# Attention scores of a hybrid diffusion backbone: 289 contraction rows per key tile packed as 128 + 128 + 33, the 33 in half of the array's rows

## The chip, the cores and the metric

The program runs on one core of one Trainium2 chip. The metric is the device time of one execution in microseconds (us). Five things work side by side on the core, each through its own queue of instructions in a fixed order: TensorE (PE in the profile; its loading of stationary weights is listed apart as PEld), VectorE (DVE), ScalarE (ACT), GpSimd (POOL), and SyncE (SP), which here only issues DMA transfers. Semaphores order them.

## The reference

Two layers (DEPTH 2) of a mixer over 2048 latent and 256 context tokens, width 1024. What matters here is the attention of each layer, 8 heads wide:

```python
q = rms_norm((rms_norm(cq, q_norm_w) @ w_uq).reshape(B, T, 8, 96), q_head_norm_w)      # 64 plain + 32 rotary
k = rms_norm(concat([k_nope, k_rope]), k_head_norm_w)                                   # 64 plain + 32 rotary
s = einsum('bqhd,bkhd->bhqk', q, k) * 96 ** -0.5      # latent queries see 2304 keys, context queries 256
p = softmax(s, axis=-1)
o = einsum('bhqk,bkhd->bqhd', p, v)
```

Before it come the projections of tokens to q, k and v and two gated convolutions; after it the output projection and the residual. In the last layer the context queries are left out.

## The kernel before

The products of this kernel take operands of type fp32r, and an fp32 value is carried as two such parts, hi and lo, so that `a*b` is summed as `hi*hi + hi*lo + lo*hi`. The work of a layer is four functions called one after the other: `tokens` (q, k, v, written to DRAM as `q_d`, `kn_d`, `kr_d`, `v_d`), `features` (the convolutions), `attention`, `project`.

`attention` walks over jobs: head by head, four blocks of 512 latent queries, and in layer 0 one more block of 256 context queries per head. A job walks over pairs of key tiles (a tile is 128 keys): 18 tiles in 9 pairs for a block of latent queries, one pair for a block of context queries. In all there are 584 pairs, 8 x 37 in layer 0 and 8 x 36 in layer 1. One pair does this:

- **scores**, L1073 to L1075: for each of the two key tiles three products into one PSUM bank `sc` (tag "a", three banks): K hi by Q hi over 97 rows (96 dimensions and a row that subtracts the query's maximum), K hi by Q lo over 96 rows, K lo by Q hi over 96 rows. 97 + 96 + 96 = 289 rows of contraction in three products, each 512 columns long (256 for context queries);
- **exponentials**, L1076 and L1077 on ScalarE: `p` in fp32 and `ph` in fp32r; L1078 on GpSimd forms `pl = p - ph`; L1085 on VectorE adds up `p`;
- **products with V**, L1100 and L1101: four per pair, issued one pair later.

Between the pairs stand the products L985 (`pmax`) that find the maxima of the queries of a later job, reduced by VectorE (L986), and, in layer 0, the modulation products of later use: L216 (`pm`), and a transpose of a row of four partitions, L220 (`pt`).

`load(h)` fetches a head: K and Q lie as tiles `[97, 18, 2, 128]` with the hi and the lo part side by side, so that one transfer of long rows on GpSimd's queue serves each of the `kn_d`, `kr_d` and `q_d` pieces. Two buffers alternate between heads; a head's transfers are called two jobs ahead.

The code names operations in a natural order, and a scheduler with a timeline model of its own then sets the order of each engine's queue, within the priorities that the code gives. TensorE runs its products in that order. In the built program each product also carries the part of the 128 x 128 array that it occupies (rows x columns): the whole array for all large products, 128 x 32 for L216 (four output columns) and 32 x 128 for L220 (four rows of contraction).

Of the kernel before, what the change touches and what calls it, by code (L numbers as in the profile page):

```python
# [9 lines left out]
F32 = mybir.dt.float32  # L10
F32R = mybir.dt.float32r
# [7 lines left out]
P = 128  # L19
# [4 lines left out]
NT = SEQ + CTX  # L24
NTT = NT // P
DEPTH = 2
H = 8
NOPE, ROPE, DV, QK = 64, 32, 64, 96
# [56 lines left out]
def trunk(ctx: ExitStack, tc: tile.TileContext, ins, out):  # L85
    nc = tc.nc
    V, S, G, PE = nc.vector, nc.scalar, nc.gpsimd, nc.tensor

    def pool(stack, name, **kw):
        return stack.enter_context(tc.tile_pool(name=name, bufs=kw.pop("bufs", 1), **kw))  # L90
# [5 lines left out]
    def psum(tag, name):  # L96
        return ps.tile([P, 512], F32, tag=tag, name=name, bufs={"a": 3, "b": 2}.get(tag, 1))
# [137 lines left out]
    def tokens(l, start):  # L235
# [353 lines left out]
        for t in range(NTT + 2):  # L589
# [8 lines left out]
            for step in (STEPS, STEPS1)[l]:  # L598
# [340 lines left out]
    def attention(l, start):  # L939
        es = ExitStack()  # L940
        tp = pool(es, f"A{l}", reuse_waits="tile")
        vp = pool(es, f"Av{l}", reuse_waits="tile")
        op = pool(es, f"Ao{l}", reuse_waits="tile", side="right")
        hp = [pool(es, f"Aa{l}", reuse_waits="tile", side="right"), pool(es, f"Ab{l}", reuse_waits="tile")]
# [3 lines left out]
        jobs = []  # L948
# [7 lines left out]
        kv = {}  # L956
        count = [0]

        def load(h):
            K = hp[h % 2].tile([97, NTT, 2, P], F32R, tag="K", name="K")  # L960
            G.dma_start(K[0:NOPE], kn_d[l][h])
            G.dma_start(K[NOPE:97], kr_d[l][h])
            Q = hp[h % 2].tile([97, NTT, 2, P], F32R, tag="Q", name="Q")
            nq_ = (SEQ if last else NT) // P
            G.dma_start(Q[0:QK, :nq_], q_d[l][h, :, :nq_])
            Vt = vp.tile([P, NTT, P], F32R, tag=f"V{h % 2}", name="Vt")
            G.dma_start(Vt, v_d[l][h])
            kv[h] = (K, Vt, Q)

        def prepare(h, s, n, k0):  # L970

            K, Vt, Q = kv[h]
            keys = [(a, min(512, NT - a)) for a in range(k0 * P, NT, 512)]
            m = mx[count[0] % 2]

            early = count[0] < NE
            count[0] += 1

            part = m
            nq = n // P  # L980
            steps = []

            def chunk(t, c, a, w):
                pm = psum("b", "pmax")
                PE.matmul(pm[:, :w], lhsT=Q[0:QK, s // P + t, 0], rhs=K[0:QK, a // P : (a + w) // P, 0], start=True, stop=True)  # L985
                V.tensor_reduce(part[:, t, c : c + 1], pm[:, :w], axis=AX.X, op=ALU.max)  # L986

            def finish():
                V.tensor_reduce(m[:, 0:nq, 96:97], part[:, 0:nq, 0 : len(keys)], axis=AX.X, op=ALU.max, negate=True)

            def turn():
                px = psum("b" if early else "e", "pmt")
                for t in range(nq):
                    PE.matmul(px[0:97, t * P : (t + 1) * P], lhsT=m[:, t, :], rhs=idr, start=True, stop=True)
                S.copy(Q[96:97, s // P : (s + n) // P, 0], px[96:97, :n].rearrange("p (a t) -> p a t", t=P))

# [11 lines left out]
        def ahead(idx, share):  # L1008

            while len(sums) <= idx + 1 and len(sums) <= len(jobs):  # L1010
                steps, ends = [], []
                for j in jobs[len(sums) - 1]:
                    a, finish, turn = prepare(*j)
                    steps += [[st] for st in a]
                    steps[-1].append(finish)
                    ends.append(turn)
                steps[-1] += ends
                queue.extend(steps)
                sums.append(sums[-1] + len(steps))
            if idx < len(jobs):  # L1020
                goal = sums[idx] + round(share * (sums[idx + 1] - sums[idx]))
                while sums[-1] - len(queue) < goal:
                    with tc.high_priority(offset=PO):
                        for st in queue.pop(0):
                            st()

        with start():
            load(0)
            ahead(0, 1)

        ready = []
# [21 lines left out]
        for idx, job in enumerate(jobs):  # L1053
            h = job[0][0]
            if job[0][1] == (1024 if h else 512) and h + 1 < H:
                load(h + 1)
            pairs = [(j, it) for j in job for it in range(j[3], NTT, 2)]
            for pi, ((h, s, n, k0), kt0) in enumerate(pairs):
                if idx == len(jobs) - 1 and pi == len(pairs) - AE:
                    mark = tc.cur_priority  # L1060
                K, Vt, Q = kv[h]
# [7 lines left out]
                scs = []  # L1069
# [240 lines left out]
```

## Time and profile before

| | |
|---|---|
| median of 3 runs | 3695.93 us (3688.89 to 3696.3) |
| the profiled execution's own time | 3695.0 us |
| its span, first to last instruction | 3693.2 us |
| PE busy | 3529.8 us (96%) |
| DVE busy | 2888.8 us (78%) |
| POOL busy | 2341.6 us (63%) |
| ACT busy | 2166.7 us (59%) |
| mean granted clock of TensorE | 0.978 |
| attention, layer 0 | about 812 to 1737 us |
| attention, layer 1 | about 2599 to 3500 us |

Busy time is the union of an engine's instruction spans. Matmuls are pipelined and their ends are modelled, so a span of 0.40 us of a product with 512 columns overlaps the next one: what a product costs in a full queue is the distance from its start to the next start. The start of a row PEld is the moment at which the weights of that product begin to be loaded.

### The profile page before, as it was taken

To read this page: it belongs to the slowest core of one execution; us is meant where nothing else is said; L and a number is where in the kernel's file an instruction comes from. 1 tells how busy PE (TensorE), PEld (TensorE's weight loads), DVE (VectorE), ACT (ScalarE), POOL (GpSimd) and SP (SyncE) were. 2 spreads that over 40 slices of the span, in tenths; PEclk is the share of its full clock that TensorE was granted. 3 is DMA by queue.
4 is the path that set the end of the run, shared out by engine and by line. 5 is a ranking of instruction groups with operands and counts; after the bars stand their busy time and mean duration, and the time that the engine had idled before them with its cause. 6 is when DMAs were issued, how large, how long until landed. Compare 5 with 4: busy or idle time off the path is not lost. (4 is left out here: it accounts for less than half of the span.)

```text
span 3693.2 us, 52810 instructions
## 1 busy us (share of the span) xinstructions
PE 3529.8 (96%) x17532; PEld 2916.9 (79%) x17532; DVE 2888.8 (78%) x5472; ACT 2166.7 (59%) x4328; POOL 2341.6 (63%) x1497
## 2 busy tenths in 40 slices
PE   7899999999999999999999989999999999998999
PEld 5787888887888787877788878887777777776777
DVE  5986977877888888888437878769988888888832
ACT  4665343247778777877445663433677777776720
POOL 4664344348888888877435654444687887877721
PEclk8999999999999999999999999999999999999999
DMA  7567333433333213312776773435232202222163
GB/s 219 171 186 205 82 107 110 113 112 78 79 79 88 61 45 82 85 58 64 232 231 207 215 213 100 114 99 125 80 76 61 41 27 61 59 61 75 43 197 114
DMA packets 394386, 411.47 MB, mean 111 GB/s; under 512 B 19168, under 2 KB 332128, under 8 KB 388960
## 3 DMA queue, kind: packets, MB, share of 16 engines
q1 hardware_dynamic: 387712, 333.87, 31.2%
q0 software_dynamic: 6400, 74.22, 8.9%
q8 instruction: 138, 2.26, 0.3%
q14 instruction: 136, 1.11, 0.1%
HBM read 266.72 MB, written 141.59 MB: 111 GB/s over the span
## 5 line engine op out<-in xcount | busy, mean ns | idle before, releaser
L1078 POOL TENSOR_TENSOR pl<-p,ph 128x1024 fp32r<-128x1024 f32 (+1 forms) x584 | 1387.2, 2397 | 276.2 <-ACT ph L1077 110.4
L986 DVE TENSOR_REDUCE mx<-pmax 128x1 fp32r<-128x512 f32 (+1 forms) x1296 | 795.1, 628 | 122.0 <-PE pmax L985 113.6
L1076 ACT ACTIVATE p<-sc 128x512 f32<-128x512 f32 x1168 | 713.4, 612 | 240.5 <-PE sc L1075 232.7
L1085 DVE TENSOR_TENSOR acc<-acc,p 128x512 f32<-128x512 f32 x1096 | 756.7, 690 | 55.9 <-ACT p L1076 29.5
L1077 ACT ACTIVATE ph<-sc 128x512 fp32r<-128x512 f32 x1168 | 703.8, 612 | 20.1 <-PE po L1100 16.2
L194 PE MATMUL pf<-hhf,wh 128*128 128x256 f32 (+1 forms) x1584 | 549.3, 348 | 18.2 <-ACT tg L867 8.4
L196 PE MATMUL pf<-hhf,wl 128*128 128x512 f32 (+1 forms) x1584 | 546.4, 347 | 4.5 <-POOL wl L191 3.7
L195 PE MATMUL pf<-hlf,wh 128*128 128x256 f32 (+1 forms) x1584 | 547.2, 346 | 0.0
L985 PE MATMUL pmax<-K,Q 96*128 96x512 f32 (+1 forms) x1296 | 465.0, 386 | 34.8 <-DVE mx L986 26.8
L1073 PE MATMUL sc<-Q,K 97*128 97x512 f32 x1168 | 476.5, 408 | 11.7 <-ACT ph L1077 9.3
L1101 PE MATMUL po<-pl,Vt 128*128 128x512 f32 x1168 | 467.9, 401 | 2.1 <-POOL pl L1078 1.8
L1074 PE MATMUL sc<-Q,K 96*128 96x512 f32 x1168 | 465.2, 398 | 0.0
L1100 PE MATMUL po<-ph,Vt 128*128 128x512 f32 x1168 | 461.9, 396 | 1.1 <-DMA Vt<-v_d 0.8
L1075 PE MATMUL sc<-Q,K 96*128 96x512 f32 x1168 | 462.4, 396 | 0.0
L191 POOL TENSOR_TENSOR wl<-wraw,wh 128x1024 fp32r<-128x1024 f32 x104 | 253.8, 2441 | 292.8 <-ACT wh L190 279.4
L747 DVE SCALAR_TENSOR_TENSOR cacc<-z,hv,cacc 128x384 f32<-128x384 f32 (+5 forms) x780 | 403.0, 561 | 14.3 <-ACT cacc L742 11.2
L194 PEld LDWEIGHTS pf<-hhf,wh 128*128 128x128 f32 x1584 | 303.7, 192 | 57.2 <-ACT wh L190 9.1
L196 PEld LDWEIGHTS pf<-hhf,wl 128*128 128x128 f32 x1584 | 303.0, 192 | 44.3 <-POOL wl L191 7.2
L985 PEld LDWEIGHTS pmax<-K,Q 96*128 96x128 f32 x1296 | 245.3, 190 | 116.9 <-DVE mx L986 58.6
L195 PEld LDWEIGHTS pf<-hlf,wh 128*128 128x128 f32 x1584 | 303.8, 192 | 36.1
L1073 PEld LDWEIGHTS sc<-Q,K 97*128 97x128 f32 x1168 | 222.2, 190 | 71.3 <-ACT ph L1077 20.0
L1075 PEld LDWEIGHTS sc<-Q,K 96*128 96x128 f32 x1168 | 224.5, 192 | 51.5
(257 smaller groups left out, 6189.0 us busy)
## 6 DMA issues: line engine op xcount, KB each, us to landing
wraw<-in_w_in SPq DMA_DIRECT2D x108, 512.0 KB
q_d<-sg SPq DMA_DIRECT2D x68, 384.0 KB
wm<-in_w_mod SPq DMA_DIRECT2D x46, 512.0 KB
v_d<-vs SPq DMA_DIRECT2D x36, 512.0 KB
kn_d<-sg SPq DMA_DIRECT2D x72, 256.0 KB
K<-kn_d POOLq DMA_DIRECT2D x16, 1152.0 KB, 8.5
Vt<-v_d POOLq DMA_DIRECT2D x16, 1152.0 KB, 14.8
o_d<-o SPq DMA_DIRECT2D x64, 256.0 KB
```

Of the source, the lines that this page charges most:

```text
L194: PE.matmul(out_, lhsT=ahi, rhs=bhi, start=first, stop=False)
L195: PE.matmul(out_, lhsT=ahi, rhs=blo, start=False, stop=False)
L196: PE.matmul(out_, lhsT=alo, rhs=bhi, start=False, stop=last)
L985: PE.matmul(pm[:, :w], lhsT=Q[0:QK, s // P + t, 0], rhs=K[0:QK, a // P : (a + w) // P, 0], start=True, stop=True)
L986: V.tensor_reduce(part[:, t, c : c + 1], pm[:, :w], axis=AX.X, op=ALU.max)
L1073: PE.matmul(sc[:, :n], lhsT=K[0:97, kt, 0], rhs=Q[0:97, qt, 0], start=True, stop=False)
L1075: PE.matmul(sc[:, :n], lhsT=K[0:QK, kt, 1], rhs=Q[0:QK, qt, 0], start=False, stop=True)
L1076: S.activation(p[:, z, :n], sc[:, :n], AF.Exp, scale=scale)
L1077: S.activation(ph[:, z, :n], sc[:, :n], AF.Exp, scale=scale)
L1078: G.tensor_tensor(pl[:, :, :n], p[:, :, :n], ph[:, :, :n].bitcast(F32), op=ALU.subtract)
L1085: V.tensor_tensor(acc[:, :n], acc[:, :n], p[:, z, :n], op=ALU.add)
L1101: PE.matmul(po[:, :n], lhsT=Vt[:, kt0 + z, :], rhs=pl[:, z, :n], start=False, stop=final and z == 1)
```

## The change

Per key tile the 289 rows are packed as two products over all 128 rows of the array (L1106) and a rest of 33 or 34 rows. For that the tiles K and Q become `[128, 18, 2, 128]`: their two planes hold two packed sets of rows instead of hi and lo. The rests of the two tiles of a pair lie in a new tile KC, that of the even tile on partitions 0 to 32 and that of the odd tile on partitions 64 to 97; the even one's partner is a new tile `qc` of 33 rows, the odd one's lies in Q. The two rests, L1102 and L1103, are given the two halves of the array's rows (64 x 128 at row 0 and at row 64) and two PSUM banks, and they open the two score sums. There are as many products as before (six per pair).

`load(h)` now copies rows to their places with 20 transfers of 512-byte pieces on SyncE's queue (16 to Q and K, 4 to KC), and a block of queries has two more for `qc`; V stays on GpSimd's queue. The row of ones becomes ones in the hi plane and zeros in the lo plane.

```diff
-            K = hp[h % 2].tile([97, NTT, 2, P], F32R, tag="K", name="K")
-            G.dma_start(K[0:NOPE], kn_d[l][h])
-            G.dma_start(K[NOPE:97], kr_d[l][h])
-            Q = hp[h % 2].tile([97, NTT, 2, P], F32R, tag="Q", name="Q")
+            K = hp[h % 2].tile([P, NTT, 2, P], F32R, tag="K", name="K")
+            KC = vp.tile([98, NTT // 2, P], F32R, tag=f"KC{h % 2}", name="KC")
+            Q = hp[h % 2].tile([P, NTT, 2, P], F32R, tag="Q", name="Q")
...
+            for r0, src, z in ((0, kn[0:63], 0), (64, kr[0:33], 0), (97, kn[63:64], 0), (63, kn[30:31], 0), (98, kn[0:30], 0)):
+                ld(k[r0 : r0 + src.shape[0], :, 0], src[:, :, z])
...
+            for r0, src, z in ((0, kr[0:32], 0), (32, kn[63:64], 0), (64, kr[0:33], 1), (97, kn[63:64], 1)):
+                ld(c[r0 : r0 + src.shape[0]], odd(src[:, :, 1])[:, :, z])
             G.dma_start(Vt, v_d[l][h])
...
+        def load_qc(h, s, n):
+
+            t = tp.tile([33, 4, P], F32R, tag="qc", name="qc", bufs=3)
+            a, e = s // P, (s + n) // P
+            nc.sync.dma_start(t.bitcast(F32)[0:32, : e - a], q_d[l][h, 64:96, a:e, 0])
+            nc.sync.dma_start(t.bitcast(F32)[32:33, : e - a], q_d[l][h, 63:64, a:e, 0])
+            qc[h, s] = t
...
-                PE.matmul(pm[:, :w], lhsT=Q[0:QK, s // P + t, 0], rhs=K[0:QK, a // P : (a + w) // P, 0], start=True, stop=True)
+                PE.matmul(pm[:, :w], lhsT=Q[:, s // P + t, 0], rhs=K[:, a // P : (a + w) // P, 0], start=True, stop=True)
...
-                for z in range(2):
-                    kt, qt = kt0 + z, slice(s // P, (s + n) // P)
-                    sc = psum("a", "sc")
-                    PE.matmul(sc[:, :n], lhsT=K[0:97, kt, 0], rhs=Q[0:97, qt, 0], start=True, stop=False)
-                    PE.matmul(sc[:, :n], lhsT=K[0:QK, kt, 0], rhs=Q[0:QK, qt, 1], start=False, stop=False)
-                    PE.matmul(sc[:, :n], lhsT=K[0:QK, kt, 1], rhs=Q[0:QK, qt, 0], start=False, stop=True)
+                scs = [psum("a", "sc") for _ in range(2)]
+                C = KC[:, kt0 // 2]
+                PE.matmul(scs[0][:, :n], lhsT=C[0:33], rhs=qc[h, s][:, : n // P], start=True, stop=False, tile_position=(0, 0))
+                PE.matmul(scs[1][:, :n], lhsT=C[64:98], rhs=Q[64:98, qt, 0], start=True, stop=False, tile_position=(64, 0))
+                for z, sc in enumerate(scs):
+                    for i in range(2):
+                        PE.matmul(sc[:, :n], lhsT=K[:, kt0 + z, i], rhs=Q[:, qt, i], start=False, stop=i == 1)
```

The scheduler sets the order anew. On TensorE, in the middle of layer 0's attention, this stands before (`sc` scores, `po` products with V, `pmax` maxima of a later job):

```order
L1073 MATMUL sc<-Q,K 128x512
L1074 MATMUL sc<-Q,K 128x512
L1075 MATMUL sc<-Q,K 128x512
L1073 MATMUL sc<-Q,K 128x512
L1074 MATMUL sc<-Q,K 128x512
L1075 MATMUL sc<-Q,K 128x512
L1101 MATMUL po<-pl,Vt 128x512
L1100 MATMUL po<-ph,Vt 128x512
L1101 MATMUL po<-pl,Vt 128x512
L1100 MATMUL po<-ph,Vt 128x512
L985 MATMUL pmax<-K,Q 128x256
```

and this after, in the middle of layer 0's attention too:

```order
L1103 MATMUL sc<-Q,KC 128x512
L1106 MATMUL sc<-Q,K 128x512 x2
L1012 MATMUL pmax<-K,Q 128x512
L1102 MATMUL sc<-qc,KC 128x512
L1106 MATMUL sc<-Q,K 128x512 x2
L1132 MATMUL po<-pl,Vt 128x512
L1131 MATMUL po<-ph,Vt 128x512
L1132 MATMUL po<-pl,Vt 128x512
L1131 MATMUL po<-ph,Vt 128x512
L1103 MATMUL sc<-Q,KC 128x512
L1106 MATMUL sc<-Q,K 128x512 x2
```

Each rest stands in front of the two full products of its own tile. Over the whole queue of TensorE, 29 of the 584 pairs have their two rests next to each other; the other 555 pairs have them apart, with products of the whole array on either side of each.

The second place is the start of attention in layer 1 on TensorE, where the last work of `features` (`pf`, and the layer norm and pointwise products `pmu`, `pva`, `ppw`) is still under way. Before:

```order
L985 MATMUL pmax<-K,Q 128x512
L985 MATMUL pmax<-K,Q 128x256
L1073 MATMUL sc<-Q,K 128x512
L1074 MATMUL sc<-Q,K 128x512
L1075 MATMUL sc<-Q,K 128x512
L196 MATMUL pf<-hhf,wl 128x512
L194 MATMUL pf<-hhf,wh 128x512
L195 MATMUL pf<-hlf,wh 128x512
```

After:

```order
L769 MATMUL pva<-tl,onr 128x264
L769 MATMUL pva<-th,onr 128x264
L769 MATMUL pva<-tl,onr 128x264
L1021 MATMUL pmt<-idr,mx_90 97x128 x4
L1012 MATMUL pmax<-K,Q 128x512 x4
L1102 MATMUL sc<-qc,KC 128x512
L1103 MATMUL sc<-Q,KC 128x512
L1106 MATMUL sc<-Q,K 128x512 x4
```

The first score of the layer moved from ahead of the last `pf` products to behind the last `pva` product.

## Rows read from the trace of the kernel before

**Rows 1.** The page: span and parts 1 (busy us, share, instructions) and 2.

```profile
span 3693.2 us, 52810 instructions
...
PE 3529.8 (96%) x17532; PEld 2916.9 (79%) x17532; DVE 2888.8 (78%) x5472; ACT 2166.7 (59%) x4328; POOL 2341.6 (63%) x1497
...
PEclk8999999999999999999999999999999999999999
```

**Rows 2.** Busy time in two stretches of attention, layer 0 and layer 1.

```profile
core 0: us, PE busy (x) PEld busy (x) DVE busy (x) ACT busy (x) POOL busy (x), PEclk, DMA share, GB/s
820.00:1660.00 840.00, 827.26 (x4063) 663.51 (x4062) 726.03 (x1338) 648.61 (x1220) 723.66 (x331) 0.99 0.30 75
2600.00:3440.00 840.00, 815.78 (x3554) 645.27 (x3553) 736.55 (x1241) 621.68 (x1184) 663.55 (x305) 0.99 0.25 59
```

**Rows 3.** PE's groups in one head of layer 0, 937.85 to 1050.62 us, shapes apart.

```profile
line engine op names shapes xcount | busy us, mean ns | idle before us <-releasers
L1073 PE MATMUL sc<-Q,K 97*128 97x512 f32 x72 | 29.3, 408 | 0.0
...
L985 PE MATMUL pmax<-K,Q 96*128 96x512 f32 x64 | 24.6, 405 | 0.1
```

**Rows 4.** Timeline of PE around a transpose L220 in layer 0's attention.

```profile
start us, us, engine line op out<-in xcount [idle before <-releaser]
1050.14 0.40 PE L985 MATMUL pmax<-K,Q 96*128 96x512 f32 x1
1050.47 0.22 PE L220 MATMUL pt<-idr,mrow 4*128 4x4 f32 x1
1050.62 0.50 PE L1073 MATMUL sc<-Q,K 97*128 97x512 f32 x1
1050.96 0.40 PE L1074 MATMUL sc<-Q,K 96*128 96x512 f32 x1
1051.19 0.40 PE L1075 MATMUL sc<-Q,K 96*128 96x512 f32 x1
1051.42 0.40 PE L1073 MATMUL sc<-Q,K 97*128 97x512 f32 x1
```

**Rows 5.** Timeline of PEld, the weight loads of the same stretch.

```profile
1050.47 0.13 PEld L220 LDWEIGHTS pt<-idr,mrow 4*128 4x128 f32 x1 [0.37 <-issue]
1050.62 0.19 PEld L1073 LDWEIGHTS sc<-Q,K 97*128 97x128 f32 x1
1050.73 0.19 PEld L1074 LDWEIGHTS sc<-Q,K 96*128 96x128 f32 x1
1050.96 0.19 PEld L1075 LDWEIGHTS sc<-Q,K 96*128 96x128 f32 x1
```

**Rows 6.** Timeline of PEld, four loads of L220 behind one another.

```profile
49.72 0.32 PEld L220 LDWEIGHTS pt<-idr,mrow 4*128 4x128 f32 x4
```

**Rows 7.** Timeline of PE, from whole-array products to L216 in fp32r parts.

```profile
1020.51 0.40 PE L1101 MATMUL po<-pl,Vt 128*128 128x512 f32 x1
1020.75 0.22 PE L216 MATMUL pm<-wmh,s 128*4 128x128 f32 x1
```

**Rows 8.** Timeline of PEld, the same stretch and where it ends.

```profile
1020.52 0.08 PEld L216 LDWEIGHTS pm<-wmh,s 128*4 128x4 f32 x1
...
1021.59 0.08 PEld L216 LDWEIGHTS pm<-wml,s 128*4 128x4 f32 x1
1021.65 0.19 PEld L985 LDWEIGHTS pmax<-K,Q 96*128 96x128 f32 x1
```

**Rows 9.** Timeline of PEld at the start, L216 in plain fp32 between `ptok` products.

```profile
45.22 0.19 PEld L195 LDWEIGHTS ptok<-wt_lo,hh 128*128 128x128 f32 x1 [0.22 <-issue]
45.61 0.09 PEld L216 LDWEIGHTS pm<-wm,rinv 128*4 128x4 f32 x2 [0.20 <-issue]
45.92 0.19 PEld L196 LDWEIGHTS ptok<-wt_hi,hl 128*128 128x128 f32 x1 [0.22 <-issue]
```

**Rows 10.** DMA queues: packets, MB, share of 16 engines' span; an issue, us to landing.

```profile
q1 hardware_dynamic: 387712, 333.87, 31.2%
...
Q<-q_d POOLq DMA_DIRECT2D x8, 1728.0 KB, 21.1
```

**Rows 11.** Issue of a transfer of 1024 pieces of 512 bytes on SP, line L203.

```profile
L203 SPq DMA_DIRECT2D wm<-in_w_mod x38: 367/384/1875, 31.6 to 1560.3; - x38
```

**Rows 12.** Timeline of PE at the start of layer 1's attention.

```profile
2598.83 0.40 PE L1073 MATMUL sc<-Q,K 97*128 97x512 f32 x1
```

**Rows 13.** Timeline of DVE there, the first step behind the `pva` products.

```profile
2621.02 0.42 DVE L782 TENSOR_SCALAR cva<-pva 128x264 f32<-128x264 f32 x1
```

More of the change, by code (lines that the diff above doesn't have):

```diff
@@ L959, in load @@
         def load(h):
-            K = hp[h % 2].tile([97, NTT, 2, P], F32R, tag="K", name="K")
-            G.dma_start(K[0:NOPE], kn_d[l][h])
-            G.dma_start(K[NOPE:97], kr_d[l][h])
-            Q = hp[h % 2].tile([97, NTT, 2, P], F32R, tag="Q", name="Q")
+            K = hp[h % 2].tile([P, NTT, 2, P], F32R, tag="K", name="K")
+            KC = vp.tile([98, NTT // 2, P], F32R, tag=f"KC{h % 2}", name="KC")
+            Q = hp[h % 2].tile([P, NTT, 2, P], F32R, tag="Q", name="Q")
+            Vt = vp.tile([P, NTT, P], F32R, tag=f"V{h % 2}", name="Vt")
@@ L964, in load @@
             nq_ = (SEQ if last else NT) // P
-            G.dma_start(Q[0:QK, :nq_], q_d[l][h, :, :nq_])
-            Vt = vp.tile([P, NTT, P], F32R, tag=f"V{h % 2}", name="Vt")
-            G.dma_start(Vt, v_d[l][h])
-            kv[h] = (K, Vt, Q)
+            k, c, q = K.bitcast(F32), KC.bitcast(F32), Q.bitcast(F32)
+            kn, kr, qd = kn_d[l][h], kr_d[l][h], q_d[l][h, :, :nq_]
+            odd = lambda d: d.rearrange("d (n two) t -> d n two t", two=2)
+            ld = nc.sync.dma_start
@@ new lines, in load @@
+            for r0, src, z in ((0, qd[0:63], 0), (64, qd[64:96], 0), (97, qd[63:64], 0), (63, qd[30:31], 1), (98, qd[0:30], 1), (96, kr[ROPE : ROPE + 1, :nq_], 1)):
+                ld(q[r0 : r0 + src.shape[0], :nq_, 0], src[:, :, z])
+            for r0, src, z in ((0, kn[0:63], 0), (64, kr[0:33], 0), (97, kn[63:64], 0), (63, kn[30:31], 0), (98, kn[0:30], 0)):
+                ld(k[r0 : r0 + src.shape[0], :, 0], src[:, :, z])
+            for r0, src, z in ((0, qd[31:96], 1), (65, qd[0:63], 0)):
+                ld(q[r0 : r0 + src.shape[0], :nq_, 1], src[:, :, z])
@@ new lines, in load @@
+            for r0, src, z in ((0, kn[31:64], 0), (33, kr[0:32], 0), (65, kn[0:63], 1)):
+                ld(k[r0 : r0 + src.shape[0], :, 1], src[:, :, z])
+            for r0, src, z in ((0, kr[0:32], 0), (32, kn[63:64], 0), (64, kr[0:33], 1), (97, kn[63:64], 1)):
+                ld(c[r0 : r0 + src.shape[0]], odd(src[:, :, 1])[:, :, z])
+            G.dma_start(Vt, v_d[l][h])
+            kv[h] = (K, Vt, Q, KC)
+        def load_qc(h, s, n):
[4 more added lines that the diff above has]
+            qc[h, s] = t
@@ L970, in prepare @@
+        qc = {}
         def prepare(h, s, n, k0):
-            K, Vt, Q = kv[h]
+            K, Vt, Q, _ = kv[h]
             keys = [(a, min(512, NT - a)) for a in range(k0 * P, NT, 512)]
@@ L1028, in attention @@
             load(0)
+            load_qc(*jobs[0][0][:3])
             ahead(0, 1)
@@ L1056, in attention @@
                 load(h + 1)
+            for j in jobs[idx][1:] + jobs[idx + 1 : idx + 2][0][:1] if idx + 1 < len(jobs) else jobs[idx][1:]:
+                load_qc(*j[:3])
             pairs = [(j, it) for j in job for it in range(j[3], NTT, 2)]
@@ L1060, in attention @@
                     mark = tc.cur_priority
-                K, Vt, Q = kv[h]
+                K, Vt, Q, KC = kv[h]
                 first, final = kt0 == k0, kt0 == NTT - 2
@@ L1068, in attention @@
                 pl = tp.tile([P, 2, 512], F32R, tag="pl", name="pl", bufs=3)
-                scs = []
-                for z in range(2):
-                    kt, qt = kt0 + z, slice(s // P, (s + n) // P)
-                    sc = psum("a", "sc")
-                    PE.matmul(sc[:, :n], lhsT=K[0:97, kt, 0], rhs=Q[0:97, qt, 0], start=True, stop=False)
-                    PE.matmul(sc[:, :n], lhsT=K[0:QK, kt, 0], rhs=Q[0:QK, qt, 1], start=False, stop=False)
-                    PE.matmul(sc[:, :n], lhsT=K[0:QK, kt, 1], rhs=Q[0:QK, qt, 0], start=False, stop=True)
+                qt = slice(s // P, (s + n) // P)
+                scs = [psum("a", "sc") for _ in range(2)]
[5 more added lines that the diff above has]
+                        PE.matmul(sc[:, :n], lhsT=K[:, kt0 + z, i], rhs=Q[:, qt, i], start=False, stop=i == 1)
                     S.activation(p[:, z, :n], sc[:, :n], AF.Exp, scale=scale)
@@ L1298 @@
     arrays["idn"] = np.eye(P, dtype=f)
-    arrays["one"] = np.ones((H, 2 * NT), f)
+    arrays["one"] = np.ascontiguousarray(np.broadcast_to(np.array([1, 0], f)[None, None, :, None], (H, NTT, 2, P)).reshape(H, 2 * NT))
     nc = bacc.Bacc("TRN2", target_bir_lowering=False, num_devices=1)
```

## The prediction

> **What bounds the kernel now.** I read first the page's span and parts 1 and 2 [rows 1]: TensorE is busy 96% of the span at a granted clock near full, the next engine, VectorE, 78%. The change touches attention alone, so the second view is the busy time in a stretch of each layer's attention [rows 2]: PE works 827.3 of 840 us in layer 0 and 815.8 of 840 in layer 1; VectorE 726 and 737, GpSimd 724 and 664, ScalarE less. The third is PE's groups within one head of layer 0 [rows 3]: before 72 score products and 64 maxima products it stood idle 0.0 and 0.1 us. So in attention PE's queue is the path, and it runs dry for 12.7 + 24.2 = 37 us in 1680. Whatever a pair gains or loses on PE is gained or lost in the time. The price of one product is the distance between starts: 1050.96, 1051.19, 1051.42, so 0.23 us for 512 columns [rows 4].
>
> **What the change removes.** Not a product: six per pair before, six after. The gain can only come from the two rests of a pair streaming at the same time, which would turn 6 x 0.23 into 5 x 0.23. For that they must follow each other on PE. In the order above they do in 29 of 584 pairs; in the other 555 a rest stands alone between products of the whole array. So 1110 rests can gain nothing, and what decides is what it costs to go from products of all 128 rows to a product in a 64-row part, and back.
>
> **The price of one visit to a row part.** The kernel before has such visits, though not for this type and size: L220, a transpose in plain fp32 that occupies 32 of the array's rows. Between whole products a load of weights normally starts with the product before it, so it is hidden: L1075's load starts at 1050.96, the start of L1074 [rows 4, 5]. Around L220 this stops. Its load starts at 1050.47, 0.33 after the start of L985 (1050.14), that is 0.10 after that product's 0.23 of streaming are over; L1073's load starts 0.15 after L220's; and L1073's load lies bare, since the next load, which starts when L1073 begins to stream, comes 0.11 later (1050.62 to 1050.73) [rows 4, 5]. From L985 to L1074 it takes 0.82 us, where two whole products take 0.46: the visit costs 0.36 us (0.35 unrounded at the least) with four columns in it. A rest has 512 columns, which add the 0.23 that it also cost before. Thus a lone rest costs 0.36 more than the product that it replaces.
>
> One part of it is open: L220's weights load fast, four of them in 0.32 us with the last one 0.13, so (0.32 - 0.13) / 3 = 0.06 each [rows 6]; the rest's are fp32r over 128 columns like L1073's, whose load took 0.11 [rows 5]. That is up to 0.05 more, so 0.35 to 0.41. I take 0.37, near the low end, because rows 6 are the only loads into a row part.
>
> The Trainium skill, "TensorEngine Tiling (Array Packing)", section "Tiling Modes", says that changing the tiling mode, not just the tile, drains TensorE. It gives no price. Rows 5 agree; rows 8 do not, as the third rival tells. By that sentence the sum is the one below; without it, that of the third rival.
>
> **The sum.**
> - 1110 lone rests x 0.37 = +411 us (0.35: 388; 0.41: 455). PE is the path, so all of it lies on it; VectorE, ScalarE and GpSimd merely get slack.
> - 29 pairs with adjacent rests: one visit, +0.37, and between nothing and 0.23 back if the two stream together; at 0.12 back, 29 x 0.25 = +7 (4 to 12).
> - PE's dry spells, 37 us in 1680 [rows 2], about 40 over both attentions, mostly waits for slower neighbours: with PE slower they shrink. I take -25 (-40 to 0).
> - The start of attention in layer 1: the first score, before at 2598.83 [rows 12], now stands behind the last `pva` product, whose result VectorE takes at 2621.02 [rows 13]. At most 22 us for PE, but `features`' own chain, then free of attention's work on VectorE, ends sooner; I take half, +11. Layer 0's start moves in the same way over less work; I take nothing, and up to another 22 for the range. So +11 (0 to 44).
> - The maxima products take 128 rows instead of 96: as many columns, the same 0.23; 0.
> - The loads. A head is now 256 x 18 pieces each for Q and K, 67 x 9 for KC and 33 x 18 for `qc`, some 10,400 pieces of 512 bytes. At the mean of the hardware queue, 0.312 x 16 x 3693 / 387,712 = 0.048 us of an engine each [rows 10], that is 31 us of all 16 engines per head, where Q alone took 21 to land before. A head lasts 112.8 us (rows 3's stretch) and the DMA engines are at 0.25 to 0.30 of their time [rows 2]. In SP's order the transfers for a head stand where its buffers come free, a whole head before their use. So they are hidden: 0. Without that cover it would be up to 31 us a head. Issuing 20 + 8 transfers at 0.38 [rows 11] takes SP 11 us per head; behind them wait only stores of results, which nobody needs before `project`. GpSimd's queue loses three issues a head, which is no bound.
>
> 411 + 7 - 25 + 11 = +404. On the profiled execution's 3695.0 us (span 3693.2, median of the runs 3695.9, so the same to 0.03%) this gives 4099: **4100 us**, 11% slower. The ends of the terms give 352 to 511, so 4047 to 4206.
>
> **The rivals.**
>
> *Second: the loads lie bare, but nothing waits for the array to run empty.* Then a visit costs the rest's load, 0.06 to 0.11, and L1106's, 0.11 [rows 5, 6]: 0.17 to 0.22 on 1139 visits, 194 to 251, middle 222. 222 - 25 + 11 = +208: 3903 (3850 to 3990). For it: L220 is plain fp32, and the 0.10 behind the stream may belong to that type. Against: loads hidden under streaming is what whole products do, so something holds the load back until the stream has ended, and that something would also hold the 0.10.
>
> *Third, the other side: changing to a row part is free for fp32r.* L216 occupies a 128 x 32 part. With fp32r parts its load starts at 1020.52, a full 0.23 ahead of its product at 1020.75, with the start of L1101 [rows 7, 8], and L985's load follows the last of them by 0.06: no stop in either direction. In plain fp32 the same line L216 does stop: its load comes 0.39 after that of a `ptok` product of 416 columns (45.22 to 45.61), and the load after two of them 0.31 later (45.61 to 45.92), where loads between whole products are never bare [rows 9]. So a stop has been seen for plain fp32 alone, in a column part and in a row part; for fp32r only a column part is on record, and it is free. If the type decides and not the part, a lone rest costs its 0.23 as before: 3695 - 29 x 0.23 + 11 = 3699 (3688 to 3732), not slower where the starts cost under 14 us. Against: a column part leaves all rows of the array in use, so that weights can be loaded as ever; a row part changes what the moving data feed, and L220 is the only row part here.
>
> *Fourth: the change does what it says.* 584 x 0.23 = 134 us less: 3695 - 134 + 11 = 3572. The Trainium skill, "TensorE: Matmul & The Clock Gate", section "Part 3: Packing small matmuls — row/col tiling", measured four row tiles at 3.07 times the speed of one; that is this mechanism. But PE runs products in the order of its queue, and there the partners stand apart.
>
> *Fifth: more than the visits.* If the stops lowered the granted clock of the stages, now 0.99 [rows 2], every product there would be dearer too: over 4200.
>
> **How the numbers follow.** First case 0.56, second 0.15, third 0.22, fourth 0.03, fifth 0.04. The time is that of the first, 4100. Alone it would reach from 4047 to 4206; with 0.44 elsewhere the range must take in the second case and the upper half of the third: 3700 to 4200, which leaves out the fourth, the fifth and half of the third. A measurement of this kernel can tell about 0.2%, or 7 us, from no change. Slower by more: first, second, fifth and half of the third, 0.86. Faster by more: the fourth and a little of the third, 0.06. Within: the remainder of the third, 0.08.
>
> **What would show it.** In the trace after: the loads of L1102 and L1103 some 0.33 us behind the start of the product before them (first case), 0.23 (second) or with it (third); the first L1106's load bare behind the rest; a head of layer 0 lasting 112.8 + 72 x 0.37 = 139 us; VectorE's share of attention falling from 0.87 to about 0.72; PE never waiting for a DMA of K, Q, KC or `qc`. The prediction is wrong if the rests' loads start with the product before them, or if PE waits for loads, which would add to any case.

## The result and the profile after

The changed kernel takes 4126.89 us (median of 4 runs, 4124.92 to 4138.65) against 3695.44 us (4 runs, 3688.89 to 3696.3): a ratio of 1.118, 95% interval 1.116 to 1.120. It is 431 us slower; forecast were 404 and 4100 us, so the sum is 27 us short. The profiled execution of the changed kernel took 4138.65 us, the slowest of its four, so readings of it add up to some 12 us more than the medians differ by.

The page of the changed kernel, span, part 1 and the clock's row of part 2, against [rows 1]:

```profile
span 4136.9 us, 53464 instructions
...
PE 3966.5 (96%) x17532; PEld 2838.2 (69%) x17532; DVE 2910.1 (70%) x5472; ACT 2232.8 (54%) x4328; POOL 2318.6 (56%) x1449
...
PEclk8999999989999999999999999997999999999999
```

As many products as before, PE as full as before, every other engine with nearly the same busy time in a longer span. So PE's queue is still the path and each turn through it lasts longer. Besides the first slice, the clock's row has two that fell below 9, an 8 and a 7; before it had none. They come back below, at the starts of attention.

Two stretches of attention, one in each layer, against [rows 2] (columns: the stretch, its length, busy time and instructions of PE, PEld, DVE, ACT and POOL, granted clock, share of the DMA engines, GB/s):

```profile
900.00:1700.00 800.00, 797.81 (x3232) 491.15 (x3231) 581.87 (x1053) 540.04 (x973) 568.83 (x246) 1.00 0.30 70
2850.00:3700.00 850.00, 844.82 (x2930) 501.79 (x2929) 606.04 (x1017) 540.29 (x978) 542.40 (x233) 0.98 0.26 60
```

PE starts 3232 products in 800 us where it started 4063 in 840, and at full clock. VectorE's share is 0.73 and 0.71 (0.72 was announced). PE's dry spells are 2.2 + 5.2 = 7 us in 1650, where they were 37 in 1680.

One visit to a row part in layer 0, the timelines of PE and then of PEld (start, duration, engine, line, shapes; x2 is two in a row under one line):

```profile
1019.89 0.39 PE L1012 MATMUL pmax<-K,Q 128*128 128x512 f32 x1
1020.21 0.50 PE L1103 MATMUL sc<-Q,KC 34*128 34x512 f32 x1
1020.63 0.73 PE L1106 MATMUL sc<-Q,K 128*128 128x512 f32 x2
1021.20 0.39 PE L1012 MATMUL pmax<-K,Q 128*128 128x512 f32 x1
...
1020.20 0.18 PEld L1103 LDWEIGHTS sc<-Q,KC 34*128 34x128 f32 x1 [0.36 <-issue]
1020.63 0.30 PEld L1106 LDWEIGHTS sc<-Q,K 128*128 128x128 f32 x2 [0.25 <-issue]
1020.97 0.19 PEld L1012 LDWEIGHTS pmax<-K,Q 128*128 128x128 f32 x1
```

This is the picture of [rows 4, 5] around L220, now with 512 columns. The rest's load does not start with L1012 at 1019.89 but at 1020.20, when that product's streaming has ended. L1106's load starts 0.43 behind it. From the start of one whole product (1019.89) through the rest and two L1106 to the next product (1021.20) it takes 1.31 us; four whole products take 4 x 0.233 = 0.93. The visit costs 0.38 here; over all visits to a lone rest of 512 columns the medians of the steps are 0.326 (product to rest), 0.428 (rest to L1106) and 0.337 (L1106 to L1106), and 0.326 + 0.428 + 0.337 - 3 x 0.233 = 0.39.

The same price in PEld's groups (busy us, mean ns of one | idle time before them, and what ended it):

```profile
L1106 PEld LDWEIGHTS sc<-Q,K 128*128 128x128 f32 x2336 | 357.0, 190 | 278.3 <-issue 270.9
```

"issue" is idle time that no semaphore explains: the loads are not late for want of data, they stand still in their own queue.

The 29 pairs whose rests are adjacent look different. PE, then PEld, of one of them:

```profile
993.00 0.22 PE L220 MATMUL pt<-idr,mrow 4*128 4x4 f32 x1
993.15 0.49 PE L1102 MATMUL sc<-qc,KC 33*128 33x512 f32 x1
993.15 0.49 PE L1103 MATMUL sc<-Q,KC 34*128 34x512 f32 x1
993.58 1.20 PE L1106 MATMUL sc<-Q,K 128*128 128x512 f32 x4
...
993.15 0.18 PEld L1102 LDWEIGHTS sc<-qc,KC 33*128 33x128 f32 x1
993.15 0.18 PEld L1103 LDWEIGHTS sc<-Q,KC 34*128 34x128 f32 x1
```

Both loads and both streams start together, and L1106 follows 0.43 later, as it does behind a single rest. So where the partners meet they do stream together, and they meet in 29 of 584 pairs. But 27 of the 29 stand right behind L220, as here, which is a row part itself and stops PE in the kernel before too.

By stage (attention is from the first score to the first `pout` product of the output projection, `project` and next `tokens` from there to the first `pf` product; us, one profiled execution each; the last two columns are experiments told below):

| stage | before | after | whole-array twin | rests last |
|---|---|---|---|---|
| to the first score, layer 0 | 812 | 834 | 839 | 816 |
| attention, layer 0 | 925 | 1116 | 929 | 979 |
| `project` and next `tokens` | 416 | 422 | 425 | 428 |
| `features` to first score, layer 1 | 446 | 484 | 486 | 469 |
| attention, layer 1 | 902 | 1078 | 857 | 902 |
| `project`, layer 1 | 193 | 204 | 201 | 203 |
| a head of layer 0, from the second on | 112.7 | 137.7 | 112.3 | 117.7 |
| a head of layer 1 | 108.4 | 133.9 | 106.5 | 110.4 |

A head is the distance between the first scores of two heads, the median over those with neither end of attention in them.

### The profile page after: what moved, and what is told of

Read it like the earlier page. It is cut to its first block, busy times and chain, and to the rows that moved or that the text cites. A ratio compares the mean times of both kernels' runs of the same rounds, so it can differ in the third digit from the quotient of the medians.

```text
span 4136.9 us, 53464 instructions
## 1 busy us (share of the span) xinstructions
PE 3966.5 (96%) x17532; PEld 2838.2 (69%) x17532; DVE 2910.1 (70%) x5472; ACT 2232.8 (54%) x4328; POOL 2318.6 (56%) x1449
## 3 DMA queue, kind: packets, MB, share of 16 engines
q1 hardware_dynamic: 554856, 416.83, 37.4%
## 4 chain that ended last, share of the span: by engine, by line
PE 41%; DVE 6%; DMA 4%; ACT 1%; issue 1%; SPq 1%; POOL 1%; DVEq 0%; POOLq 0%; ACTq 0%
PE sc L1106 10%; PE sc L1103 3%; PE sc L1102 3%; PE pmax L1012 3%; PE po L1132 3%; PE po L1131 3%; PE pout L194 2%; PE pout L196 2%; PE pout L195 2%; PE pf L194 2%; PE pf L196 2%; PE pf L195 2%; DMA wraw<-in_w_out 1%; DVE mx L1013 1%; DVE cacc L747 1%
## 5 line engine op out<-in xcount | busy, mean ns | idle before, releaser
L1013 DVE TENSOR_REDUCE mx<-pmax 128x1 fp32r<-128x512 f32 (+1 forms) x1296 | 803.4, 632 | 466.6 <-PE pmax L1012 459.0
L1107 ACT ACTIVATE p<-sc 128x512 f32<-128x512 f32 x1168 | 696.4, 596 | 555.5 <-PE sc L1106 553.2
L1106 PE MATMUL sc<-Q,K 128*128 128x512 f32 x2336 | 848.6, 449 | 0.0
L1108 ACT ACTIVATE ph<-sc 128x512 fp32r<-128x512 f32 x1168 | 683.1, 594 | 29.5 <-PE po L1131 18.4
L1106 PEld LDWEIGHTS sc<-Q,K 128*128 128x128 f32 x2336 | 357.0, 190 | 278.3 <-issue 270.9
L1012 PE MATMUL pmax<-K,Q 128*128 128x512 f32 (+1 forms) x1296 | 468.3, 387 | 14.2 <-DVE mx L1013 5.1
L1012 PEld LDWEIGHTS pmax<-K,Q 128*128 128x128 f32 x1296 | 246.0, 190 | 96.0 <-DVE mx L1013 29.8
L1103 PE MATMUL sc<-Q,KC 34*128 34x512 f32 (+1 forms) x584 | 292.7, 501 | 9.8 <-ACT ph L1108 8.5
L1102 PE MATMUL sc<-qc,KC 33*128 33x512 f32 (+1 forms) x584 | 292.4, 501 | 3.1 <-DMA qc<-q_d 2.9
L1132 PEld LDWEIGHTS po<-pl,Vt 128*128 128x128 f32 x1168 | 221.3, 189 | 49.8 <-POOL pl L1109 3.8
```

The lines of the kernel that those rows point to most:

```text
L1012: PE.matmul(pm[:, :w], lhsT=Q[:, s // P + t, 0], rhs=K[:, a // P : (a + w) // P, 0], start=True, stop=True)
L1106: PE.matmul(sc[:, :n], lhsT=K[:, kt0 + z, i], rhs=Q[:, qt, i], start=False, stop=i == 1)
L1132: PE.matmul(po[:, :n], lhsT=Vt[:, kt0 + z, :], rhs=pl[:, z, :n], start=False, stop=final and z == 1)
```

## The experiments

The theory: a product in a row part between whole-array products makes PE run empty and load bare, 0.37 us each time, and nothing else matters. The rivals: the loads, the queues and the starts carry the loss; the size of the part or the plain fp32 type decides; the number of row products counts, not that of the visits.

**The whole-array twin: both rests as products of 98 rows.** Same loads (and one more per head and per block of queries), as many products, and again 29 pairs with their rests adjacent, but no score in a row part; the added rows hold other rows of K and Q, which enter the sums.

```diff
-PE.matmul(scs[0][:, :n], lhsT=C[0:33], rhs=qc[h, s][:, : n // P], start=True, stop=False, tile_position=(0, 0))
-PE.matmul(scs[1][:, :n], lhsT=C[64:98], rhs=Q[64:98, qt, 0], start=True, stop=False, tile_position=(64, 0))
+PE.matmul(scs[0][:, :n], lhsT=C[0:98], rhs=qc[h, s][0:98, : n // P], start=True, stop=False)
+PE.matmul(scs[1][:, :n], lhsT=C[0:98], rhs=Q[0:98, qt, 0], start=True, stop=False)
```

> The changed kernel with both rests as products of the whole array: their weights and moving data are read over 98 rows (rows 33 to 63 of KC and 33 to 97 of qc are filled with other data by one more transfer each), so the scores are not those of the reference. Everything else stays: six products per pair, the packing, the loads of 512-byte pieces, and the order, in which 29 pairs again have adjacent rests. Theory (each visit to a row part costs 0.39 us of TensorE, as the trace of the changed kernel shows: 0.326 + 0.430 + 0.337 between starts where three whole products take 0.70): nearly all of the loss goes, 3700 to 3740 us, what is left above 3695 being the later starts of attention. Rival (the loads, the new order or the smaller overlap at the stage borders cost the time): it stays above 4000 us.

Measured: 3736.51 us (4 runs, 3730.72 to 3746.58), ratio 1.012 (1.010 to 1.015). PE's timeline where the rest is now a whole product (L1103):

```profile
1019.91 0.39 PE L1013 MATMUL pmax<-K,Q 128*128 128x512 f32 x1
1020.14 0.40 PE L1103 MATMUL sc<-qc,KC 98*128 98x512 f32 x1
1020.37 0.63 PE L1107 MATMUL sc<-Q,K 128*128 128x512 f32 x2
1020.84 0.39 PE L1013 MATMUL pmax<-K,Q 128*128 128x512 f32 x1
```

From 1019.91 to 1020.84 is 0.93 us, four products at 0.233; the same four steps take 1.31 with a row part. Of the 431 us the row parts hold 390. The twin itself is 42 us above the kernel before, with no score in a row part; of this the sum had nothing but the +11 of the starts.

**Only the even tile's rest in a row part.** L1102 as in the change, L1103 as in the twin.

```diff
-PE.matmul(scs[1][:, :n], lhsT=C[64:98], rhs=Q[64:98, qt, 0], start=True, stop=False, tile_position=(64, 0))
+PE.matmul(scs[1][:, :n], lhsT=C[0:98], rhs=Q[0:98, qt, 0], start=True, stop=False)
```

> The changed kernel with the rest of the odd tile as a product of the whole array (98 rows, so the scores are not those of the reference), that of the even tile still in the upper half of the rows: 584 visits where the changed kernel has 1139. Theory (a price per visit): 584 x 0.39 = 228 us above the kernel with no row part, about 3930 to 3970 us, half of the loss. Rival (the price is one of the kernel, the loads or the order, not of the visits): within 1% of the changed kernel's 4127 us or of the kernel without row parts.

Measured: 3949.76 us in one execution, the twin and 213; 213 / 584 = 0.365 us a visit. A head of layer 0 lasts 126.0 us, the twin's 112.3 and 13.7, and 13.7 / 37 = 0.37. Half the visits, about half (55%) of the 390 us.

**Parts of 32 rows.** The same two rests over 32 rows each (the last row of the even and the last two of the odd rest are left out).

```diff
-... lhsT=C[0:33], rhs=qc[h, s][:, : n // P], ... tile_position=(0, 0))
-... lhsT=C[64:98], rhs=Q[64:98, qt, 0], ... tile_position=(64, 0))
+... lhsT=C[0:32], rhs=qc[h, s][0:32, : n // P], ... tile_position=(0, 0))
+... lhsT=C[64:96], rhs=Q[64:96, qt, 0], ... tile_position=(64, 0))
```

> The changed kernel with the rests cut to 32 rows, one and two rows less, so that they occupy 32 x 128 parts instead of 64 x 128 (the left-out rows make the scores slightly wrong). Theory (leaving and entering the whole array costs, whatever the part, and the load of 128 fp32r columns takes 0.11 us in any part): 4110 to 4150 us, as the changed kernel. Rival (a 32-row part loads its weights in 0.06 us, as the transposes L220 of the kernel before do): 0.05 less on each of 1136 visits, 4060 to 4085 us.

Measured: 4112.65 us in one execution, within 0.4% of the change; heads of 137.2 and 132.0 us. The same stretch as above:

```profile
900.00:1700.00 800.00, 797.84 (x3240) 490.61 (x3241) 582.89 (x1055) 542.07 (x975) 569.61 (x247) 1.00 0.31 71
```

3240 products against 3232: the size of the part does not set the price. This matters for the bounds of the forecast: a load of fp32r weights into 32 rows is not cheaper, so the low end, taken from L220's loads [rows 6], did not apply to these rests.

**The old visit without its part.** In the kernel before, L220's transpose is replaced by a plain fp32 product over 97 rows, the added ones zeros, which occupies the whole array: the type stays, the part goes.

```diff
-            PE.transpose(out=pt[:, 4 * i : 4 * i + 4], in_=row[:, i * P : (i + 1) * P], identity=idn[0:4, 0:4])
+            if row.shape[0] > 4:
+                PE.matmul(pt[:, 4 * i : 4 * i + 4], lhsT=row[:, i * P : (i + 1) * P], rhs=idn[0 : row.shape[0], 0:4], start=True, stop=True)
+            else: ...
```

> The kernel before with its own visits to a row part in layer 0's attention taken out: the 32 transposes L220 of rows on four partitions become products over 97 partitions with zeros on the others, in the whole array. Theory (the visit costs, not the plain fp32 type): some 32 x 0.33 = 10 us less, ratio 0.997. Rival (the stop around L220 belongs to plain fp32 or to its wait for VectorE): no change, 0.999 to 1.001.

Measured: 3691.49 us (12 runs), ratio 0.9999 (0.9985 to 1.0013): the saving looked for is not there. The trace tells why, and answers the question all the same. PE, then PEld, around the product that took L220's place (L221):

```profile
990.71 0.64 PE L988 MATMUL pmax<-K,Q 96*128 96x512 f32 x2
991.18 0.28 PE L221 MATMUL pt<-idr,mrow 97*128 97x4 f32 x2
991.32 0.48 PE L1083 MATMUL sc<-Q,K 97*128 97x512 f32 x1
991.64 0.40 PE L1084 MATMUL sc<-Q,K 96*128 96x512 f32 x1
...
990.95 0.42 PEld L221 LDWEIGHTS pt<-idr,mrow 97*128 97x128 f32 x2
```

L221's first load starts at 990.95 with the second L988 (which starts 0.23 behind 990.71), 0.23 ahead of its product: no stop. L220's load came 0.33 behind such a product [rows 4, 5]. Nor is it the transpose: in the kernel before the transposes `psum_t` (L1113), which take the whole array, begin to load at 3508.00, with the product before them (3507.99). So at L220 it is the row part that stops PE, not the plain fp32 type, which closes the third rival's best argument; in the column part of L216 the type does make a difference [rows 8, 9]. From that L988 to L1084 it takes 0.69 us against 0.82 there: 0.13 saved, not 0.36, since this product runs in two passes, each with a load of its own, and has so few columns that the loads lie bare. 32 x 0.13 = 4 us is too little to measure.

**All rests adjacent, banks in pairs: a dead end.** To make every pair's rests meet, the two score banks were taken as one tile of two banks, two such tiles in PSUM; a control gave the kernel before the same layout.

```diff
-            scs = [psum("a", "sc") for _ in range(2)]
+            scs = psum_pair("sc")        # one tile [P, 2, 512]; tag "a" two of these, tag "e" joined to "a" and "b"
```

> A control for the next run: the kernel before with the scores of a pair in one tile of two PSUM banks, two such tiles, which together take the four banks of the tags a and e of all stages; the products are those of the kernel before. Both theories: slower than before by the coarser release of banks, 3700 to 3800 us; it serves as the base.

> The changed kernel with the same PSUM layout as the control. Its pair of banks comes free at once, and so the two rests of all 584 pairs stand next to each other on TensorE, as the change intends. Theory (adjacent rests stream together, and a visit costs 0.39 us whether one or two rests are in it): per pair 0.39 - 0.23 = 0.16 us more than the control, 94 us, and some 20 to 30 us at the starts of attention: about 115 us above the control, so the change loses even as it is meant. Rival A (adjacent rests are worth it: the two halves save 0.23 and the visit is cheaper): 50 to 130 us below the control. Rival B (they stream one after the other): 584 x 0.39, 230 us above the control.

Measured: the control 4793.96 us, ratio 1.298 (1.295 to 1.301); the change in this layout 4819.82, ratio 1.304 (1.301 to 1.308). Expected were 3700 to 3800 for the control. The same stretch of attention in the control:

```profile
1100.00:1900.00 800.00, 714.90 (x3095) 513.09 (x3093) 554.79 (x1018) 501.60 (x927) 546.17 (x253) 0.95 0.24 59
```

In the change with this layout PE is busy for 714.02 of the same 800 us. So PE is idle for 85 and 86 us, of which 49 and 50 are scores that wait for ScalarE's exponentials (L1088 and L1119) to release a bank. PE's queue alone is no longer the path, and the difference of 26 us prices nothing; none of the three differences named ahead (about 115 slower, 50 to 130 faster, 230 slower) came out. No conclusion on adjacency is drawn from this pair.

**All rests adjacent, the rests last.** The three single banks stay. The four whole products open the sums, the rests close them, and the first rest is made to depend on the last whole product, so that both banks are already held when the rests come. 583 of 584 pairs then have their rests adjacent in PE's queue.

```diff
-PE.matmul(scs[0] ... C[0:33] ... start=True, stop=False ...)      # both rests, ahead of the loop
-PE.matmul(scs[1] ... C[64:98] ... start=True, stop=False ...)
 for z, sc in enumerate(scs):
     for i in range(2):
-        PE.matmul(sc[:, :n], ... start=False, stop=i == 1)
+        whole = PE.matmul(sc[:, :n], ... start=i == 0, stop=False)
+rest = PE.matmul(scs[0] ... C[0:33] ... start=False, stop=True ...)
+tc.add_manual_dep(rest.ins, whole.ins.name, ...)
+PE.matmul(scs[1] ... C[64:98] ... start=False, stop=True ...)
```

> The changed kernel with a pair's four whole products first (the first of each bank opens the sum) and the two rests last, behind an added dependence of the first rest on the last whole product: 583 of the 584 pairs of rests stand adjacent in TensorE's queue, each with both banks already open, and the buffers of scores are 3 as before. Theory (a row part costs a stop where whole products meet it, 0.09 us to enter, bare loads of 0.11 us on both sides, 0.09 us to leave, so 0.39 us a visit, and two adjacent rests stream together): an adjacent visit costs 0.39 - 0.23 = 0.16 us against the kernel before, so 584 x 0.16 = 93 us, on top of the 42 us that the whole-array twin of the change already costs: 3830 us (3800 to 3860). Heads of layer 0 with no start in them come to 112.3 + 36 x 0.16 = 118 us. Rival 1 (the rests do not really stream together, the stop is paid and both streams too): 584 x 0.39 = 228 us, 3965 us. Rival 2 (it is the number of row products that costs, not the number of visits): as the changed kernel, 4127 us, less nothing. Rival 3 (adjacent rests hide their loads too and pay back the stop, as the change was meant to): at or below the twin, 3700 to 3736 us.

Measured: 3796.48 us (4 runs, 3795.33 to 3798.06), ratio 1.027 (1.025 to 1.030): 330 us less than the change, from the order of the products alone, and still 101 more than the kernel before. PE's timeline of one visit:

```profile
1021.52 0.63 PE L1104 MATMUL sc<-Q,K 128*128 128x512 f32 x2
1022.08 0.49 PE L1105 MATMUL sc<-qc,KC 33*128 33x512 f32 x1
1022.09 0.50 PE L1107 MATMUL sc<-Q,KC 34*128 34x512 f32 x1
1022.52 0.50 PE L1012 MATMUL pmax<-K,Q 128*128 128x512 f32 x1
1022.85 0.39 PE L1134 MATMUL po<-pl,Vt 128*128 128x512 f32 x1
1023.09 0.39 PE L1133 MATMUL po<-ph,Vt 128*128 128x512 f32 x1
1023.32 0.39 PE L1134 MATMUL po<-pl,Vt 128*128 128x512 f32 x1
1023.55 0.39 PE L1133 MATMUL po<-ph,Vt 128*128 128x512 f32 x1
```

Whole products start 0.70 / 3 = 0.233 apart (1022.85 to 1023.55). From 1021.52 to 1022.85 there are five products, two L1104, two rests and L1012, in 1.33 us; five whole ones take 1.165. So the visit costs 0.39 as ever, gives back 0.23 for the second rest, and ends 0.16 dearer than not packing at all. Over the 581 visits of this form the median is the same 0.16. 584 x 0.16 = 93 us is close to what both attentions together lose against the twin: 979 - 929 and 902 - 857, 50 + 45 = 95. By the heads, which leave the starts out, it is less: 5.4 us for 37 pairs and 3.9 for 36, 0.15 and 0.11 a pair. The total of 3796 lies 4 us below the range expected, since the other side of the comparison moved too: with the whole products first, the first scores no longer wait for KC and `qc`, and the first score of layer 0 comes 23 us earlier than in the twin, that of layer 1 17 to 18 us earlier in its stage. Rivals with both streams paid (3965) or no gain from meeting (4127) fall; so does the one in which meeting pays back the stop (3700 to 3736).

**The first head's loads on GpSimd's queue.** The twin, with the loads of each layer's first head and first queries issued by GpSimd, as the kernel before does, to find its 42 us.

```diff
-            ld = nc.sync.dma_start
+            ld = (nc.sync if h else nc.gpsimd).dma_start      # and the same for the first block's qc
```

> The whole-array twin of the change (both rests as products of 98 rows of the whole array, 3736.5 us), with the loads of each layer's first head and of its first group's queries issued by GpSimd, as in the kernel before, instead of SyncE, where they stand behind the stores of the features. Nothing else differs. Theory (the 42 us that the twin costs are SyncE's queue at the two starts of attention: the first head's many pieces stand behind stores there and land late): most of it comes back, 3695 to 3710 us, with the first score of layer 0 near 815 us and features to first score of layer 1 near 450 us. Rival (the number of pieces and their one-partition rows cost it, whichever queue issues them, or the thin stretch lowers the clock all the same): 3730 to 3745 us.

Measured: 3774.64 us, ratio 1.021 (1.018 to 1.024), 38 us more than the twin; both expectations fall. GpSimd's timeline at the start of layer 0's attention:

```profile
837.55 2.36 POOL L191 TENSOR_TENSOR wml<-wm,wmh 128x1024 fp32r<-128x1024 f32 x1 [15.79 <-ACT wmh L190]
839.85 0.66 POOL L983 DMA_DIRECT2D KC<-kr_d  x1
...
841.81 2.98 POOL L983 DMA_DIRECT2D KC<-kn_d  x2
...
845.39 0.56 POOL L991 DMA_DIRECT2D qc<-q_d  x1
```

The transfers to KC stand behind an instruction that waits 15.8 us for ScalarE, those to `qc` behind them, and the first score of layer 0 moves from 839 to 865 us; PE's last wait before it is 4.8 us for `qc`. So SyncE as such is not at fault. It fits both runs that what counts is what the last transfers that the first score needs stand behind, in whichever queue; but PE's order at the start changed with them and was not held fixed, so this is not shown by itself. In the changed kernel these transfers stand behind a store that SyncE issues at 823.15:

```profile
823.15 0.51 SPq L811 DMA_DIRECT2D y_d<-sgcl  x1
823.76 0.63 SPq L983 DMA_DIRECT2D KC<-kr_d  x1
824.45 0.77 SPq L983 DMA_DIRECT2D KC<-kn_d  x1
825.27 0.78 SPq L983 DMA_DIRECT2D KC<-kr_d  x1
826.09 0.69 SPq L983 DMA_DIRECT2D KC<-kn_d  x1
826.89 0.40 SPq L991 DMA_DIRECT2D qc<-q_d  x1
827.34 0.62 SPq L992 DMA_DIRECT2D qc<-q_d  x1
```

By that time the first score of the kernel before was 11 us in the past (812.5). The kernel with the rests last shows the same from the other side: its first scores need neither KC nor `qc`, and start at 816.

## Why the prediction was right, step by step

**The bound.** Right: PE's queue is the path before and after, and 390 of 431 us are products that start later in it.

**1110 lone rests x 0.37 = +411.** Right in mechanism and nearly in size. A lone visit costs 0.39, so +433. The missing 0.02 is the choice near the low one of the two bounds, 0.35 by L220's loads [rows 6] and 0.41 by L1073's [rows 5]: the rests' loads cost the same over 32 rows as over 33 and 34, so L220's were no measure for them. Why L220's take less (plain fp32, four rows) is open. The parts of the visit in the trace are 0.09 from the end of the stream to the rest's load, 0.20 around the rest's own stream (0.43 - 0.23), and 0.10 bare load of L1106. The 0.20 can be read as 0.11 of bare load, as L1073's, and 0.09 on the way out; this split is an estimate. The sign announced for this case, the load 0.33 behind the product before it, stands there. A head of layer 0 lasts 137.7 us, where 139 was announced with 72 visits; by the whole queue it has 67 lone rests.

The Trainium skill, "TensorEngine Tiling (Array Packing)", section "Tiling Modes", has a change of the tiling mode drain TensorE. The runs agree for every row part, 32 or 64 rows, plain fp32 or fp32r; they still disagree for the fp32r column part of L216, whose loads keep ahead [rows 7, 8].

**29 adjacent pairs, +7.** Too high by some 8 us. The 0.12 that I put back for streaming together was half of what it is, 0.23; and I counted a whole visit for each pair, where 27 of them stand right behind L220. From L220's start to that of the second L1106 behind it the median of the 27 is 0.92 us, where the twin takes 0.95 for the same steps: 27 x -0.03 = -1 us.

**PE's dry spells, -25.** Right: 37 us in 1680 became 7 in 1650, some -30 over both attentions.

**The starts, +11, and a term that was left out.** 433 - 1 - 30 = 402; the medians differ by 431 and the profiled executions by 444, which leaves 29 to 42 us.

Of the 444, 17 (6 + 11) lie by the table in the two stages that begin with `project`. "The change touches attention alone", the prediction says, and it has no term for them. But the scheduler's new order reaches them. Of the eight casts in each layer to `woh`, the output projection's weights, three and four start ahead of the layer's first `pout` product in the kernel before; in the changed kernel it is one in each layer (1949.1 and 3932.3, the products 1950.2 and 3933.4). PE, which never waited for `woh` before, now does:

```profile
PE pout L194 <- ACT woh L190: 11.3, 10, 3.3
```

The twin shows the same (one cast in each layer, 9 and 8 us by the table), so the row parts are not the reason. Why the casts moved is open.

The other 12 to 25 us are for the starts. They lie within the bounds of 0 to 44 but above the +11, so this term was somewhat small. Where it went wrong: I costed the first score's place in PE's order and took layer 0 at nothing, and did not ask where in SyncE's queue the transfers to KC and `qc` stand. PE's waits name it in one small row, for L1102:

```profile
PE sc L1102 <- DMA qc<-q_d: 2.9, 2, 2.0
```

Only 2.9 us in two waits, while PE had other work; the rest shows as a thin stretch ahead of the first score and, behind it, a lower clock. Layer 0 in the changed kernel (columns as above):

```profile
810.00:820.00 10.00, 10.00 (x51) 8.27 (x49) 7.61 (x15) 4.14 (x7) 0.45 (x1) 1.00 0.11 39
820.00:834.00 14.00, 10.03 (x31) 5.51 (x30) 11.59 (x21) 1.13 (x3) 2.80 (x4) 0.83 0.75 245
834.00:845.00 11.00, 10.78 (x21) 5.85 (x21) 3.12 (x5) 4.49 (x8) 3.60 (x2) 0.50 0.61 167
845.00:860.00 15.00, 15.00 (x53) 8.99 (x52) 6.60 (x11) 6.83 (x13) 10.47 (x5) 0.50 0.86 175
```

and the second of these stretches in the kernel before:

```profile
820.00:834.00 14.00, 13.97 (x61) 10.85 (x60) 13.18 (x24) 12.75 (x24) 13.98 (x9) 1.00 0.98 248
```

In 820 to 834 PE starts 31 products where it started 61, and then works 26 us at half clock (0.50, the 1.2 GHz level): about 13 us lost. Layer 1 shows the same, 35 us at half clock, about 17 us lost, behind a stretch in which PE was busy 11.6 of 15 us:

```profile
2840.00:2855.00 15.00, 11.62 (x37) 6.63 (x35) 13.53 (x29) 3.08 (x5) 3.67 (x4) 0.72 0.81 250
2855.00:2870.00 15.00, 14.55 (x28) 7.91 (x28) 12.78 (x18) 8.53 (x17) 6.65 (x3) 0.50 0.07 18
2870.00:2890.00 20.00, 20.00 (x43) 12.39 (x43) 7.48 (x13) 7.11 (x13) 8.84 (x6) 0.50 0.02 7
```

Both losses are estimates, and together they are more than the 12 to 25. Against them stands another thing that the sum does not have: in the midst of attention the kernel before shows 37 us at half clock (a mean clock of 0.99 from 920 to 1737 and 0.98 from 2800 to 3500), the changed kernel none (1.00 from 920 to 1950 and from 3050 to 3933), which gives back some 18 us by the same reckoning. What part of the starts is clock and what is waiting was not tested apart.

**The maxima products and the loads, 0.** Right. The maxima products keep their step of 0.23 us. The hardware queue moved 554,856 packets instead of 387,712 [rows 10] in nearly the same share of DMA time per stretch (0.30 and 0.26), and within the heads PE waited for none of them. The announced sign "PE never waits for a DMA" holds but for the two starts (2.9 us for `qc`, and 4.6 us for K ahead of layer 1).

**The rivals.** The second (bare loads, no stop) falls with the rest's load 0.31 to 0.33 behind the product before. The third (a row part is free for fp32r) falls with the stop in front of the fp32r rests and with the twin, and its argument from the type with the old visit without its part. The fourth (the change does what it says) is right that adjacent rests stream together, but between whole-array products they still lose 0.16 us a pair. The fifth (a clock falling with the stops) is not seen: 1.00 in the midst of attention with 409 visits in the 800 us from 900 on. The clock does fall, but at the starts, for another reason.

## What to carry to other kernels

A product in a row part of the array between whole-array products has a fixed price, here 0.39 us, 1.7 whole products of 512 columns: before packing, count the visits in the order that the queue will really have, and pack only where each visit saves more than that. One pair per visit does not (0.23 saved); by these numbers two pairs per visit would, by 2 x 0.233 - 0.39 = 0.08 us, which is an estimate and asks for four open banks, and was not tried. And for a change of the loads ask at the start of the stage, not in its midst, what the last transfer needed by the first product stands behind in its queue, and whether the scheduler's new order delays stages that the change does not touch (17 us here). No version with the packed rows that was tried here beats the kernel before.

## What was not expected of the hardware

- Two products in the two 64-row halves do not follow each other: they load (both at 993.15) and stream together, 3 ns apart in the median of 581 visits. The Trainium skill, "TensorE: Matmul & The Clock Gate", section "Part 3: Packing small matmuls — row/col tiling", has four row tiles at 3.07 times one; here two cost the streaming of one, and the stop around them, 0.39 us, takes the gain away.
- The stop costs the same for parts of 32 and of 64 rows with 512 columns (heads of 137.2 and 137.7 us), and nearly as much with 4 columns in plain fp32 ([rows 4], 0.36 against 0.39); a whole-array plain fp32 product has none.
- SyncE needs 0.63 to 0.78 us to issue each of the first four transfers to KC and 0.62 for the first one-row transfer to `qc`, where a transfer of 1024 pieces took 0.38 [rows 11].
- Behind the thin stretches ahead of the first scores (PE busy 10.0 of 14 us and 11.6 of 15) PE worked 26 and 35 us at half clock, through stretches in which it was busy again without a pause (15.00 of 15 us, 20.00 of 20).
